# The triangular inverse of a recurrent layer on blocks of 16 instead of 32, completed by two small products

## The chip, the cores and the metric

The kernel runs on one core of a Trainium2 chip. The metric is the device time of one execution in microseconds (us), as a median of runs. A core has five engines that work through their own instruction lists in order and wait for each other by semaphores: PE (TensorE, matrix products), DVE (VectorE), ACT (ScalarE), POOL (GpSimd) and SP, which here only issues DMAs.

## What is computed

The reference is a two-layer encoder trunk on 512 positions of width 1024: layer A (RWKV-7 time mixing with 12 heads of 64, beside a four-head attention into memory tokens), layer B (chunked attention beside the same memory attention), a gated channel mixer after each, all in float32. The change lies in the recurrence of layer A:

```
def step(state, inp):
    r_t, w_t, k_t, v_t, a_t, b_t = inp
    sa = jnp.einsum('bhvk,bhk->bhv', state, a_t)
    state = (state * w_t[:, :, None, :] + sa[..., None] * b_t[:, :, None, :]
             + v_t[..., None] * k_t[:, :, None, :])
    return state, jnp.einsum('bhvk,bhk->bhv', state, r_t)
```

The kernel doesn't step through positions. It cuts the 512 positions into 8 chunks of 64 and solves each chunk at once. Within a chunk the terms `sa` depend on each other through a strictly triangular 64x64 matrix L, so that the inverse T of (identity minus L) is needed, for each chunk and each head.

## The kernel before

**Pairs and stages.** The 12 heads are worked on in 6 pairs, numbered 0 to 5; a pair's two heads lie in the upper and the lower 64 partitions. Each pair passes three generators: `prepare` (its three projections, decay, keys, and the inverse), `front` (the chunk's matrices, masked) and `back` (the completed inverse, the chunk recurrence, the output norm). A stage weaves `back` of one pair, `front` of the next and `prepare` of the one after: `weave` always continues the generator that is least far along by its share of an estimated cost, where each `yield` names a cost in ns (and perhaps a pause). What comes out of it is then put in order for each engine by a scheduler, and that order is fixed in the program. The sixth pair has no further `prepare` beside it: in the last weave its `front` and `back` run beside `back` of the fifth pair, the memory attention (`q_mem`, `mA`) and the first output projections (`out_ahead`).

**The inverse.** In `keys`, L643 makes the 64x64 matrices of all chunks in PSUM. For each head the two 32x32 blocks on the diagonal go to DRAM (`Lc`, L648 and L649) and come back with one block per partition, in four copies for four groups of columns (`Lr`, L653). DVE then solves for the inverse of all blocks at once by forward substitution over 31 steps (L656 to L668): for the first eight steps one instruction for each column group (L661), later two instructions (L666 into `Xu`, L668 into the tile `Xs`). The result goes through DRAM again (L671, L674) into the diagonal blocks of the tile `Tt`. `back` completes `Tt` from 32 to 64: it transposes blocks on DVE (`Tl`, L775), multiplies 32x32 tiles on PE (L780, into `X5`, L784; L794) and copies the off-diagonal block into `Tt` (L798). L804 uses the finished `Tt`.

**Around it.** `norm` statistics of heads go through `head_rsqrt`: L549 on PE, small instructions (L221 to L225) and L555 on DVE, L558 on PE. `front` multiplies (L716), masks (L719 on DVE), and copies on ACT (L744, L733). Weights are loaded in full precision (`wraw`, two buffers, L180 on SP) and split into two parts of lower precision: L169 on ACT, and the rest either by L175 on DVE or, between the first and the last stage, by L172 on ACT and an adding DMA on POOL's queue (L173). The dense products take both parts (L198, L199, L202), three matmuls for each block of 128 inputs. SP issues all other DMAs from one queue, in order.

In the last weave the tiles of `other_tiles` reuse buffers for the sixth pair's `back`: `AR`, and before the change `Lr` (for `MQ`) and `Xs` (for the split weight `g2h`, `g2l`).

Of the kernel before, what the change touches and what calls it, by code (L numbers as in the profile page):

```python
# [18 lines left out]
P = 128  # L19
# [20 lines left out]
for _n, _c in _VEC:  # L40
# [5 lines left out]
        ("m1", 128), ("i64", 64), ("x0", 256)]  # L46
# [8 lines left out]
def _constants():  # L55
    f = np.float32
    c = np.zeros((P, NCST), f)

    def put(name, a):
        o, n = COFF[name]  # L60
        c[:, o:o + n] = a

    i = np.arange(P)
    same = (i[:, None] // 64) == (i[None, :] // 64)
    put("ident", np.eye(P, dtype=f))
    put("ones_d", np.full((P, 2), 1.0 / 1024, f))
# [10 lines left out]
    put("x0", (np.arange(32)[None, None, :] == 4 * np.arange(8)[None, :, None] + (i // 32)[:, None, None])  # L77
        .astype(f).reshape(P, 256))
    return c
# [32 lines left out]
def trunk_kernel(ctx, tc, A, out):  # L112
# [275 lines left out]
    Tts = [lp.tile([P, NCH, 64], F32, name=f"Tt{n_}") for n_ in range(3)]  # L388
# [27 lines left out]
    xs = [kt_("Lr", (P, 32, 32))[:].rearrange("p a b -> p (a b)").rearrange("p (m s) -> p m s", m=2),  # L416
# [16 lines left out]
    for t_ in Tts:  # L433
        for h in range(2):
            GP.memset(t_[h * 64 + 32:h * 64 + 64, :, 0:32], 0.0)
# [28 lines left out]
    norm_rho(acc, rho[:])  # L464

# [99 lines left out]
    def prepare(i, T):  # L565
# [54 lines left out]
        def keys():  # L620
# [23 lines left out]
            Lc = kt_("Lc", (P, NCH, 32))  # L644
# [6 lines left out]
            Lr = kt_("Lr", (P, 32, 32))  # L651
            for g in range(4):
                nc.sync.dma_start(Lr[g * 32:g * 32 + 32], d1[:].rearrange("u c i s -> (u c) i s"))  # L653
            X = kt_("Xs", (P, 8, 32))
            V.tensor_copy(X[:].rearrange("p m i -> p (m i)"), C("x0"))
            for q in range(31):  # L656
                k, n = q // 4 + 1, 31 - q
                L1 = Lr[:, q + 1:, q:q + 1]
                if k <= 2:
                    for m in range(k):  # L660
                        V.scalar_tensor_tensor(X[:, m, q + 1:], L1[:, :, 0], X[:, m, q:q + 1], X[:, m, q + 1:],  # L661
                                               op0=ALU.mult, op1=ALU.add)
                    continue
                u = kt_("Xu", (P, 80))
                uv = u[:, 0:k * n].rearrange("p (m i) -> p m i", i=n)
                V.tensor_tensor(uv, L1.rearrange("p i o -> p o i").to_broadcast([P, k, n]),  # L666
                                X[:, 0:k, q:q + 1].to_broadcast([P, k, n]), op=ALU.mult)
                V.tensor_tensor(X[:, 0:k, q + 1:], X[:, 0:k, q + 1:], uv, op=ALU.add)  # L668
            d2 = dp.tile([4, NCH, 8, 4, 32], F32, name="d2", tag="d2", bufs=2)
            for g in range(4):  # L670
                nc.sync.dma_start(d2[:, :, :, g, :].rearrange("u c m i -> (u c) m i"), X[g * 32:g * 32 + 32])  # L671
            for u in range(4):
                rw = slice(u * 32, u * 32 + 32)
                nc.sync.dma_start(Tt[rw, :, u % 2 * 32:u % 2 * 32 + 32], d2[u].rearrange("c m g i -> (m g) c i"))  # L674
# [31 lines left out]
    def front(i, T):  # L706
        v, KB, AR, Tt = c3(T["v"][:]), T["KB"], T["AR"], T["Tt"]
# [41 lines left out]
        yield 800  # L749
        T.update(Rq=Rq, ML=ML, VT=VT)  # L750

    FRONT_COST = 2 * 1000 + 1000 + 800
# [6 lines left out]
    def other_tiles():  # L759
# [3 lines left out]
        mq = kt_("Lr", (P, 32, 32))[:].rearrange("p a b -> p (a b)").rearrange("p (c t) -> p c t", c=8)  # L763
        g = kt_("Xs", (P, 2, P), dt=F32R)
# [161 lines left out]

    def told(g, n):
# [3 lines left out]
    def ahead():  # L931
# [6 lines left out]
           (chain(front(b_, Ts[b_]), back(b_, Ts[b_], dst_mix, other_tiles, lambda: "back" in over)),  # L938
# [338 lines left out]
```

## Time and profile before

| | |
|---|---|
| median of 3 runs | 1378.8 us (1378.46 to 1378.82) |
| profiled execution: time, span | 1377.77 us, 1376.0 us |
| mean granted clock of PE | 0.987 |
| busy: PE, DVE, ACT, POOL | 1319.7 (96%), 826.9 (60%), 611.6 (44%), 34.1 (2%) us |
| where the recurrent layer lies | the first 345 us or so of the span |

All times below are in us from the start of the profiled span, unless marked ns. A row of a timeline gives start, duration, engine, source line, operation, the tiles written and read, shapes, the number of instructions merged into the row, and in brackets for how long the engine stood idle before and what ended that. A row of waits gives the waiting engine and line, what it waited for, the sum, the count and the longest. A matmul's duration contains its way through the array, so the spacing of starts tells what a matmul costs, not its duration.

### The profile page before, as it was taken

The page shows a single profiled execution, that of the slowest core. Times are in us where ns is not written, and L with a number is a line of the kernel's source. Part 1 is how long each engine was busy: PE and PEld are TensorE (multiplying, and loading weights), DVE is VectorE, ACT ScalarE, POOL GpSimd, SP SyncE. Part 2 cuts the span into 40 slices and gives each one's busy share as a digit, 9 for nine tenths or more (in the row PEclk, how much of TensorE's full clock was granted, in tenths as well). Part 3 has the DMA queues.
Part 4 walks back from the last instruction along what each step waited for, and adds up shares of the span by engine and source line. Part 5 has one row for each costly group of instructions (what it writes and reads, how often), then busy time and mean ns, then how long its engine had stood idle before and what let it go on. Part 6 is the DMA issues. An engine that isn't in the chain of part 4 may idle for free. (4 is left out here: it accounts for less than half of the span.)

```text
span 1376.0 us, 20868 instructions
## 1 busy us (share of the span) xinstructions
PE 1319.7 (96%) x8266; PEld 1071.2 (78%) x8266; DVE 826.9 (60%) x1752; ACT 611.6 (44%) x1022; POOL 34.1 (2%) x55
## 2 busy tenths in 40 slices
PE   6999999995999999999999999999999999999996
PEld 5777777774688888888888878786788888888886
DVE  7876789774666555565333667657665565563324
ACT  5556555552444333333222566657443333332321
POOL 3000000000000000000000000000000000000000
PEclk9999999997999999999999999999999999999998
DMA  5276544451042223223232422223223222222332
GB/s 181 83 208 136 109 108 110 99 142 42 24 146 92 92 94 106 92 93 102 84 98 85 152 91 74 90 92 99 93 92 103 96 93 102 98 88 85 104 94 75
DMA packets 63506, 139.18 MB, mean 101 GB/s; under 512 B 24624, under 2 KB 28336, under 8 KB 63408
## 3 DMA queue, kind: packets, MB, share of 16 engines
q1 hardware_dynamic: 60672, 127.89, 29.3%
q0 software_dynamic: 2736, 9.96, 4.2%
q8 instruction: 65, 1.06, 0.3%
q14 instruction: 33, 0.27, 0.1%
HBM read 131.01 MB, written 6.82 MB: 100 GB/s over the span
## 5 line engine op out<-in xcount | busy, mean ns | idle before, releaser
L175 DVE TENSOR_TENSOR wlo<-wraw,whi 128x1024 fp32r<-128x1024 f32 x183 | 218.9, 1197 | 128.4 <-PE psd L202 118.3
L169 ACT CAST whi<-wraw 128x1024 fp32r<-128x1024 f32 (+1 forms) x202 | 207.6, 1029 | 153.3 <-PE psd L199 38.5
L198 PE MATMUL psd<-r1h,whi 128*128 128x512 f32 x336 | 136.6, 407 | 1.3 <-ACT whi L169 1.2
L198 PE MATMUL psf<-r2h,whi 128*128 128x512 f32 x352 | 137.2, 390 | 0.0
L198 PE MATMUL psf<-r1h,whi 128*128 128x512 f32 x352 | 137.2, 390 | 0.0
L199 PE MATMUL psf<-r1l,whi 128*128 128x512 f32 x352 | 137.1, 390 | 0.0
L199 PE MATMUL psf<-r2l,whi 128*128 128x512 f32 x352 | 137.1, 390 | 0.0
L199 PE MATMUL psd<-r1l,whi 128*128 128x512 f32 x336 | 134.1, 399 | 0.0
L202 PE MATMUL psd<-r1h,wlo 128*128 128x512 f32 x336 | 92.5, 403 | 3.1 <-DMA wlo<-in_wA_dram 3.1
L199 PE MATMUL psd<-f3l,whi 128*128 128x512 f32 (+1 forms) x238 | 88.7, 377 | 0.0
L198 PE MATMUL psd<-f3h,whi 128*128 128x512 f32 (+1 forms) x238 | 88.6, 377 | 0.0
L358 DVE TENSOR_TENSOR tmp<-psf,rho 128x512 f32<-128x512 f32 x44 | 30.4, 692 | 94.7 <-PE psf L202 94.7
L202 PE MATMUL psf<-r1h,wlo 128*128 128x512 f32 x352 | 87.0, 389 | 0.0
L202 PE MATMUL psf<-r2h,wlo 128*128 128x512 f32 x352 | 86.9, 389 | 0.0
L198 PE MATMUL psd<-r2h,whi 128*128 128x512 f32 (+1 forms) x200 | 77.6, 392 | 0.1
L198 PEld LDWEIGHTS psd<-r1h,whi 128*128 128x128 f32 x336 | 63.8, 190 | 17.4 <-issue 2.4
L199 PE MATMUL psd<-r2l,whi 128*128 128x512 f32 (+1 forms) x200 | 76.4, 385 | 0.8 <-DVE r2l L215 0.8
L202 PEld LDWEIGHTS psf<-r1h,wlo 128*128 128x128 f32 x352 | 66.1, 188 | 13.7
L202 PEld LDWEIGHTS psf<-r2h,wlo 128*128 128x128 f32 x352 | 66.1, 188 | 13.7
L199 PEld LDWEIGHTS psf<-r1l,whi 128*128 128x128 f32 x352 | 66.1, 188 | 13.6
L198 PEld LDWEIGHTS psf<-r2h,whi 128*128 128x128 f32 x352 | 66.1, 188 | 13.7
L199 PEld LDWEIGHTS psf<-r2l,whi 128*128 128x128 f32 x352 | 66.1, 188 | 13.6
(352 smaller groups left out, 2429.2 us busy)
## 6 DMA issues: line engine op xcount, KB each, us to landing
wraw<-in_ffn_in_dram SPq DMA_DIRECT2D x88, 512.0 KB, 3.3
wraw<-in_ffn_out_dram SPq DMA_DIRECT2D x32, 448.0 KB, 3.3
wraw<-in_wA_dram SPq DMA_DIRECT2D x20, 512.0 KB, 4.3
wlo<-in_wA_dram POOLq DMA_DIRECT2D x17, 512.0 KB, 7.7
wraw<-in_w_out_dram SPq DMA_DIRECT2D x16, 512.0 KB, 3.8
wraw<-in_ffn_out_dram SPq DMA_DIRECT2D x16, 512.0 KB, 4.1
wraw<-in_wB_dram SPq DMA_DIRECT2D x8, 512.0 KB, 3.4
Lr<-d SPq DMA_DIRECT2D x24, 128.0 KB, 5.5
```

The lines of the kernel that those rows point to most:

```text
L169: SC.copy(hi[:, :n], raw)
L175: V.tensor_tensor(lo[:, :n], raw, hi[:, :n], op=ALU.subtract)
L198: PE.matmul(ps, wh[:, j * P:(j + 1) * P], ah, start=start and n == 0, stop=False)
L199: PE.matmul(ps, wh[:, j * P:(j + 1) * P], al, start=False, stop=False)
L202: PE.matmul(ps, wl[:, j * P:(j + 1) * P], act(k)[0], start=False, stop=stop and n == len(ks) - 1)
L358: V.tensor_tensor(v[:], pv[:], rho[:], op=ALU.mult)
```

## The change

The diagonal blocks that are solved by substitution shrink from 32 to 16 rows. The half-size inverses are put together to 32 by two products per pair, at the end of `front`:

- `Lr` has four blocks of 16 per 32-block and head in place of copies for four column groups: `Lr[P, 16, 16]`, filled by four DMAs of rows of 16 numbers (64 bytes); two copies for two column groups.
- The substitution has 15 steps: four with one instruction per column group (six instructions), eleven with two. `X` becomes a fixed tile of 48 columns, of which 16 on either side stay zero, so that a 16-block goes out as a row of 32 with zeros beside it. The start values `x0` take 128 columns instead of 256.
- The way back from DRAM feeds a second tile `Tc` beside `Tt`: eight DMAs in turn, instead of four. `Lc` and `Tc` live on until `front` (`Lc` with two buffers).
- `front` transposes `Tc` on DVE (`Tn`), multiplies `Lc` by the lower block (L770), copies (`Y`, L772), multiplies by the transposed upper block (L778) and copies the off-diagonal 16x16 blocks into `Tt` in four pieces (L781).
- The cost of `front` for the weave grows by 1600 ns; a pause of 6000 ns stands between `front` and `back` of the last pair. `other_tiles` takes `KB` and `Lr` in place of `Lr` and `Xs`. At the start, `Tts` become one tile whose first parts hold the input x for a while, so its clearing on POOL moves behind the input's norm.

```diff
-            Lr = kt_("Lr", (P, 32, 32))
-            for g in range(4):
-                nc.sync.dma_start(Lr[g * 32:g * 32 + 32], d1[:].rearrange("u c i s -> (u c) i s"))
-            X = kt_("Xs", (P, 8, 32))
-            V.tensor_copy(X[:].rearrange("p m i -> p (m i)"), C("x0"))
-            for q in range(31):
-                k, n = q // 4 + 1, 31 - q
+            Lr = kt_("Lr", (P, 16, 16))
+            for g in range(2):
+                for b_ in range(2):
+                    o, bs = g * 64 + b_ * 32, slice(b_ * 16, b_ * 16 + 16)
+                    nc.sync.dma_start(Lr[o:o + 32], d1[:, :, bs, bs].rearrange("u c i s -> (u c) i s"))
+            V.tensor_copy(X[:, :, 16:32], C("x0").rearrange("p (m i) -> p m i", i=16))
+            for q in range(15):
+                k, n = q // 2 + 1, 15 - q
...
-            d2 = dp.tile([4, NCH, 8, 4, 32], F32, name="d2", tag="d2", bufs=2)
-            for g in range(4):
-                nc.sync.dma_start(d2[:, :, :, g, :].rearrange("u c m i -> (u c) m i"), X[g * 32:g * 32 + 32])
+            d2 = dp.tile([4, NCH, 2, 8, 2, 32], F32, name="d2", tag="d2", bufs=2)
+            for g in range(2):
+                for b_ in range(2):
+                    o = g * 64 + b_ * 32
+                    nc.sync.dma_start(d2[:, :, b_, :, g].rearrange("u c m i -> (u c) m i"),
+                                      X[o:o + 32, :, 16 - b_ * 16:48 - b_ * 16])
+            Tc = kt_("Tc", (P, NCH, 32))
             for u in range(4):
-                rw = slice(u * 32, u * 32 + 32)
-                nc.sync.dma_start(Tt[rw, :, u % 2 * 32:u % 2 * 32 + 32], d2[u].rearrange("c m g i -> (m g) c i"))
+                rw, sr = slice(u * 32, u * 32 + 32), d2[u].rearrange("c b m g i -> (b m g) c i")
+                nc.sync.dma_start(Tc[rw], sr)
+                nc.sync.dma_start(Tt[rw, :, u % 2 * 32:u % 2 * 32 + 32], sr)
+            T.update(Lc=Lc, Tc=Tc)
...
+        Tn = kt_("Tn", (P, NCH, 32))
+        V.transpose(Tn[:].rearrange("p c s -> p (c s)"), Tc[:].rearrange("p c s -> p (c s)"))
+        ps = ps_s((P, 8, 16))
+        for c in range(8):
+            for u in range(4):
+                rw = slice(u * 32, u * 32 + 32)
+                PE.matmul(ps[rw, c], Lc[rw, c], Tc[rw, c, 16:32], start=True, stop=True, tile_position=(u * 32, u * 32))
+        Y = kt_("Y", (P, NCH, 16))
+        SC.copy(Y[:], ps[:])
+        yield 800, 600
+        ps = ps_s((P, 8, 16))
+        for c in range(8):
+            for u in range(4):
+                rw = slice(u * 32, u * 32 + 16)
+                PE.matmul(ps[rw, c], Tn[rw, c, 0:16], Y[rw, c], start=True, stop=True, tile_position=(u * 32, u * 32))
+        for u in range(4):
+            rw = slice(u * 32, u * 32 + 16)
+            SC.copy(Tt[rw, :, u % 2 * 32 + 16:u % 2 * 32 + 32], ps[rw])
+        yield 800
...
-           (chain(front(b_, Ts[b_]), back(b_, Ts[b_], dst_mix, other_tiles, lambda: "back" in over)),
+           (chain(front(b_, Ts[b_]), later(6000), back(b_, Ts[b_], dst_mix, other_tiles, lambda: "back" in over)),
```

The change also moves instructions in the fixed order of each engine. Three places matter below. A row gives the line, the operation, the tile written, the tiles read, the shape and the number of equal rows in a run.

The first is PE in the last weave, where the last dense product of the memory queries (L202) ends and the sixth pair's inverse is first needed. Before:

```order
L202 MATMUL psd<-r1h,wlo 128x512 x6
L830 MATMUL psl<-ML,VT 64x64 x8
L202 MATMUL psd<-r1h,wlo 128x512 x2
L780 MATMUL pss<-AR,ML 32x32
L788 MATMUL pss<-VT,ML 64x64 x12
L780 MATMUL pss<-AR,ML 32x32 x15
L788 MATMUL pss<-VT,ML 64x64 x4
L804 MATMUL pss<-VT,Tt_93 64x128 x8
L794 MATMUL pss<-Tt_94,AR 32x32 x16
```

And after, from the same six L202 on; L814 stands for L780, L838 for L804, L849 for L815, L855 for L821:

```order
L202 MATMUL psd<-r1h,wlo 128x512 x6
L770 MATMUL pss<-Tc,Lc 32x16
L864 MATMUL psl<-ML,VT 64x64 x8
L202 MATMUL psd<-r1h,wlo 128x512 x2
L770 MATMUL pss<-Tc,Lc 32x16 x31
L778 MATMUL pss<-Y,Tn 16x16 x32
L838 MATMUL pss<-VT,Tt_92 64x128 x8
L849 MATMUL pss<-ML,W 64x128 x16
L855 MATMUL pss<-VT,ML 64x64 x16
L814 MATMUL pss<-AR,ML 32x32 x16
```

The two new products stand where the sixth pair's L780 stood, and three groups of the fifth pair's `back` (L838, L849, L855) now stand ahead of L814, which had followed L780.

The second place is DVE at the head norm of the fourth pair, just before the last weave (`hra` and `rsq` are the norm's, `v` and `bon` belong to the sixth pair's `prepare`). Before, with the substitution only after the masking:

```order
L225 SCALAR_TENSOR_TENSOR rsq<-rsq_3841,rsq 128x8
L555 COPY tmp<-rsq 128x512
L856 TENSOR_TENSOR tmp<-tmp,pss 128x512
L858 TENSOR_TENSOR tmp<-tmp,bon 128x512
L719 TENSOR_TENSOR ML<-pss,cst 128x4x128
L867 TENSOR_TENSOR tmp<-tmp,psl 128x512
L719 TENSOR_TENSOR ML<-pss,cst 128x4x128 x2
L661 SCALAR_TENSOR_TENSOR Xs<-Lr,Xs 128x31
```

After, at the same norm; L560 stands for L555, L732 for L719:

```order
L224 SCALAR_TENSOR_TENSOR rsq_3980<-rsq_3980,hra 128x8
L667 SCALAR_TENSOR_TENSOR Xs<-Lr,Xs 128x15
L667 SCALAR_TENSOR_TENSOR Xs<-Lr,Xs 128x13
L667 SCALAR_TENSOR_TENSOR Xs<-Lr,Xs 128x14
L667 SCALAR_TENSOR_TENSOR Xs<-Lr,Xs 128x12
L667 SCALAR_TENSOR_TENSOR Xs<-Lr,Xs 128x13
L225 SCALAR_TENSOR_TENSOR rsq<-rsq_3980,rsq 128x8
L714 TENSOR_TENSOR bon<-pss,v 128x512
L667 SCALAR_TENSOR_TENSOR Xs<-Lr,Xs 128x12
L223 TENSOR_TENSOR rsq_3980<-rsq 128x8
L672 TENSOR_TENSOR Xu<-Lr,Xs 128x33
L224 SCALAR_TENSOR_TENSOR rsq_3980<-rsq_3980,hra 128x8
```

The substitution has moved ahead of the end of the norm: 12 of its instructions stand before L560. Its last three stand behind the fourth masking.

The third place is ACT in the last weave (`X` and `AR` are the off-diagonal blocks of the fifth and the sixth pair, `Lr` there the split weight of the sixth pair's `back`), after the change:

```order
L172 ACTIVATE wlo<-wraw 128x1024
L818 COPY X<-pss 32x256 x2
L891 ACTIVATE tmp<-tmp,vec 128x512
L823 COPY VT<-pss 128x512
L214 CAST Lr<-tmp 128x128
L757 COPY VT<-pss 128x512 x2
L832 COPY Tt_92<-pss 32x8x32 x2
L746 COPY ML<-pss 128x8x64 x2
L839 COPY W<-pss 128x256
L841 COPY VT<-pss 64x256 x2
```

Before, the cast of that weight (then into `Xs`) stood behind eight more rows, the last of them four casts of the mixed heads (`r1h`), and none of the copies here stood behind it.

More of the change, by code (lines that the diff above doesn't have):

```diff
@@ L387, in trunk_kernel @@
     E = lp.tile([P, NCH, 65], F32, name="E")
-    Tts = [lp.tile([P, NCH, 64], F32, name=f"Tt{n_}") for n_ in range(3)]
+    Tt3 = lp.tile([P, 3, NCH, 64], F32, name="Tt3")
+    Tts = [Tt3[:, n_] for n_ in range(3)]
     om = lp.tile([P, 18], F32, name="om")
@@ L432, in trunk_kernel @@
     GP.memset(E[:, :, 0:1], 1.0)
[L433 to L435 removed]
+    X = lp.tile([P, 8, 48], F32, name="Xs")
+    for o in (0, 32):
+        GP.memset(X[:, :, o:o + 16], 0.0)
     hact = pair_of(r1h, r1l)
@@ L464, in trunk_kernel @@
     norm_rho(acc, rho[:])
+    for t_ in Tts:
+        for h in range(2):
+            GP.memset(t_[h * 64 + 32:h * 64 + 64, :, 0:32], 0.0)
     GP.memset(acc[:], 1.0)
```

31 lines of the change are left out of this document (17 added, 14 removed).

## The prediction

> **What bounds the kernel now.** The page gives PE 96% busy, so I looked for the place where it is not: first at the busy time by stretch, then at PE's waits, then at the timelines around the longest. The columns of the first view are busy time and count of each engine, then PE's granted clock.
>
> ```profile
> core 0: us, PE busy (x) PEld busy (x) DVE busy (x) ACT busy (x) POOL busy (x), PEclk, DMA share, GB/s
> 98.00:102.00 4.00, 4.00 (x23) 3.10 (x22) 2.02 (x6) 1.04 (x1) 0.13 (x1) 0.61 1.06 263
> 270.00:300.00 30.00, 28.82 (x334) 21.87 (x329) 22.35 (x78) 15.79 (x27) 1.72 (x2) 1.00 0.43 87
> 326.00:331.00 5.00, 4.62 (x82) 4.08 (x82) 0.67 (x2) 1.31 (x3) 0.00 (x0) 0.50 0.11 18
> engine line waited for: us in total, times, longest us
> PE pss L780 <- DVE AR L775: 14.7, 1, 14.7
> PE psd L202 <- DMA wlo<-in_wA_dram: 3.1, 1, 3.1
> PE psl L835 <- DVE W L836: 1.8, 3, 0.7
> ```
>
> In the stages of pairs 0 to 4 PE is the limit (28.82 of 30); what leaves DVE there is worth little, and what comes to PE is paid in full. Only between 311 and 326 does PE stand still, once, 14.7 us, for the last pair's inverse. Afterwards it works at clock 0.50 until 331, so some 2.3 of those 5 us are lost too. DVE and SP show what it waited for:
>
> ```profile
> 290.65 0.17 DVE L849 TENSOR_SCALAR hra<-pss 128x8 f32<-128x8 f32 x1 [1.49 <-PE pss L549]
> 294.54 0.43 DVE L555 COPY tmp<-rsq 128x512 f32<-128x512 f32 x1
> 300.96 1.59 DVE L661 SCALAR_TENSOR_TENSOR Xs<-Lr,Xs 128x31 f32<-128x31 f32 x9
> 302.46 0.69 DVE L719 TENSOR_TENSOR ML<-pss,cst 128x512 f32<-128x512 f32 x1
> 316.26 1.23 DVE L175 TENSOR_TENSOR wlo<-wraw,whi 128x1024 fp32r<-128x1024 f32 x1
> 318.37 0.20 DVE L666 TENSOR_TENSOR Xu<-Lr,Xs 128x28 f32<-128x28 f32 x1
> 319.88 0.17 DVE L668 TENSOR_TENSOR Xs<-Xs,Xu 128x8 f32<-128x8 f32 x1
> 327.20 0.43 DVE L775 STREAM_TRANSPOSE AR<-Tt 32x256 f32<-32x256 f32 x1 [0.97 <-DMA Tt<-d]
> 320.08 2.52 SPq L671 DMA_DIRECT2D d<-Xs  x4
> 324.09 1.82 SPq L674 DMA_DIRECT2D Tt<-d  x4
> ```
>
> The substitution runs from 300.96 to 320.05. Its result then goes out to DRAM and back: first issue 320.08, read back from 324.09 (4.0 later), second transpose at 327.20.
>
> Below, names of the changed kernel's lines stand with those they had: L563 was L558, L560 was L555, L732 was L719, L757 was L744, L814 was L780, L818 was L784.
>
> **DVE's part.** Six substitutions before:
>
> ```profile
> L666 DVE TENSOR_TENSOR Xu<-Lr,Xs x138: 164/258/302, 84.9 to 319.7; 128x60 f32<-128x60 f32 x18, 128x66 f32<-128x66 f32 x12, 128x69 f32<-128x69 f32 x6, 128x63 f32<-128x63 f32 x6
> L668 DVE TENSOR_TENSOR Xs<-Xs,Xu x138: 166/220/239, 85.7 to 319.9; 128x60 f32<-128x60 f32 x18, 128x66 f32<-128x66 f32 x12, 128x69 f32<-128x69 f32 x6, 128x63 f32<-128x63 f32 x6
> L661 DVE SCALAR_TENSOR_TENSOR Xs<-Lr,Xs x72: 227/254/273, 78.0 to 303.6; 128x27 f32<-128x27 f32 x12, 128x26 f32<-128x26 f32 x12, 128x25 f32<-128x25 f32 x12, 128x24 f32<-128x24 f32 x12
> ```
>
> A sixth is 23 x 0.258 + 23 x 0.220 + 12 x 0.254 = 14.0 us. After, 11 steps of two instructions on 8 to 36 columns (0.17 to 0.21 by the rows at 318.37 and 319.88) and 6 single ones (at most 0.23): 22 x 0.19 + 6 x 0.23 = 5.6. So 8.4 us leave DVE in each pair. By themselves I cost them at nothing, since PE covers them in five of six stages (DVE 22.35 of 30 beside PE's 28.82).
>
> **PE's part.** Two new products per pair, each 32 calls on four 32x32 tiles along the diagonal; an fp32 call is two matmul instructions (16 calls show as x32), so 64 instructions each. The nearest rows:
>
> ```profile
> 256.38 1.15 PE L788 MATMUL pss<-VT,ML 64*64 64x64 f32 x32 [0.34 <-DVE ML L719]
> 257.46 0.69 PE L794 MATMUL pss<-Tt,X 32*32 32x32 f32 x32
> 258.08 0.50 PE L198 MATMUL psd<-r1h,whi 128*128 128x512 f32 x1
> 258.42 0.40 PE L199 MATMUL psd<-r1l,whi 128*128 128x512 f32 x1
> 258.65 0.39 PE L198 MATMUL psd<-r1h,whi 128*128 128x512 f32 x1
> 268.53 0.27 PE L740 MATMUL pss<-cst,AR 64*64 64x64 f32 x2
> 269.46 0.23 PE L742 MATMUL pss<-cst,v 64*64 64x64 f32 x2
> 269.62 1.15 PE L821 MATMUL pss<-VT,ML 128*64 128x64 f32 x32
> ```
>
> L794, on two tiles, takes 0.62 (257.46 to 258.08) for 32. On 64x64 tiles, two tiles take 1.08 for 32 (L788), four take 1.09 for 64 (L740 with L742, 268.53 to 269.62): four tiles work side by side. So 64 instructions on four tiles cost about 0.6, at most 1.24 if only two overlap, at least 0.3 if 16 columns instead of 32 halve it. The next dense product starts 0.34 after the first instead of 0.23: 0.11 more for each switch. A pair pays 2 x 0.7 = 1.4 (0.8 to 2.7). Pairs 0 to 4: **+7.0** (4 to 13.5).
>
> The Trainium skill speaks against this, in "TensorE: Matmul & The Clock Gate", section "Wait — 56ns, not 53.3ns?": start-to-start never falls under about 25 ns, however narrow the matmul. By it a pair would pay 3.2 us in place of 1.4. L794's 0.62 for 32 is 19 ns, so this trace already lies under that floor, on two tiles.
>
> ACT gets five small copies per pair, at most 0.37 each (two of 32x256 take 0.75, L798 below): 1.8 us beside 15.79 of 30 busy, hidden in the stages by PE's work and counted in the tail. The halved constant and the zeroing at the start are hidden as well: POOL's sums there wait 13.6 us for ACT, and the clearing that has moved fits into that wait.
>
> ```profile
> L462 POOL TENSOR_TENSOR Rq<-Rq,tmp 128x512 f32<-128x512 f32 x3 | 5.6, 1854 | 13.8 <-ACT tmp L460 13.6
> 256.83 0.69 DVE L719 TENSOR_TENSOR ML<-pss,cst 128x512 f32<-128x512 f32 x1
> 273.48 1.64 PE L202 MATMUL psd<-r1h,wlo 128*128 128x512 f32 x6
> 275.16 1.06 ACT L172 ACTIVATE wlo<-wraw 128x1024 fp32r<-128x1024 f32 x1 [1.05 <-PE psd L202]
> 82.90 1.22 DVE L175 TENSOR_TENSOR wlo<-wraw,whi 128x1024 fp32r<-128x1024 f32 x1
> 84.15 5.66 SPq L180 DMA_DIRECT2D wraw<-in_wA_dram  x3
> ```
>
> **New waits.** In four stages the order puts 12 substitution instructions ahead of L560 (L555 before), which PE's L563 needs. L555 ended at 294.97, just as PE got there. 12 x 0.18 (L661's nine in 1.59) is 2.2; two transposes of 0.43 have left the place, and PE has two dense products more to do first (0.46): up to 0.9, at least nothing. I take 0.5, **+2.0**. The first new product should wait for no DMA in the stages. Take pair 4: its substitution now ends just after the second masking (256.83 + 0.69, so 257.7), Tc lands 8.5 later by the tail's steps below, at 266.2, and L770 stands behind the six L202 that end at 275.0: 9 us of lead. If Tc were that late, everything on PE would stand behind L770, and DVE's queue behind the transpose Tn. Four more DMA issues a pair (1.8 us of SP, by L674's row) stand ahead of a weight load; that load needs a weight buffer which ACT's L172 frees only at 276.2, so they cost nothing, and 1.8 where that cover is gone.
>
> **What relief brings.** The 3.1 us wait on wlo, followed by clock 0.61 for 4 us (1.6 lost), belongs to a weight whose load SP issued at 84.15, just when DVE's L175, amid the first substitution, had read the buffer (82.90 + 1.22). Fewer instructions stand ahead of that now: nothing to 4.7, and I take a little under the middle, **-2.0**. Other waits for DVE such as L835's 1.8: **-1.5** (nothing to 3).
>
> **The tail**, on the old time axis. The substitution starts after the rsqrt row, about 291.5, and its last three instructions stand behind the fourth masking (L732, before L719, ended 303.15): end about 304. That is 16 us sooner. Three things eat of it:
>
> ```profile
> 301.70 1.07 ACT L744 COPY VT<-pss 128x512 f32<-128x512 f32 x2 [2.59 <-PE pss L742]
> 310.96 0.73 PE L202 MATMUL psd<-r1h,wlo 128*128 128x512 f32 x2
> 326.38 0.28 PE L780 MATMUL pss<-AR,ML 32*32 32x32 f32 x2 [14.69 <-DVE AR L775]
> 328.06 1.05 PE L780 MATMUL pss<-AR,ML 32*32 32x32 f32 x30
> 332.14 0.75 ACT L798 COPY Tt<-pss 32x256 f32<-32x256 f32 x2
> ```
>
> First, ACT's cast of a weight into Lr (L214) now stands ahead of the VT copies (301.70 before) and must wait until the substitution has read Lr: copies at 304.3, PE 2.3 late, dense work done at about 314.3 instead of 311.7. Secondly, the way through DRAM: 304.5 + 4.0, the seventh of eight issues (6 x 0.455), landing 1.75: Tc there at 313.0, so L770 finds it ready and ends at 315. Thirdly, the transpose Tn stands on DVE behind L912 (which needs the dense work, 0.7), two splits (0.6 each) and L175 (1.23): done at 317.9; L778 then ends at 318.5. Copies (four, at most 0.37 each) and two transposes lie beside 2.6 us of the former pair's products, with about 1 us of wait in them: L814 at 322.1. Before, its place was 328.06, with those 2.6 still to do and 1.5 still to lose at half clock. Some 2 us of new waits follow, as there is less left to fill them: 6.0 + 2.6 + 1.5 - 2.0 = **-8.1** (-3 to -14), pair 5's products included.
>
> **Sum:** 7.0 + 2.0 - 2.0 - 1.5 - 8.1 = -2.6 on the profiled execution's 1377.77. The median of the three runs, 1378.8, stands 1.0 above that, so 1376.2 on the median's scale.
>
> **Rivals.**
> *Dear small products, slower:* if tiles overlap only by two, a pair pays 2.7: 6.5 more over five pairs and 1.3 in the tail, 1384.0. The sum turns positive from 1.8 us a pair on. For it: no row here has four tiles of 32 rows, or 16 columns. Against it: L740 with L742. By the Trainium skill's 25 ns (the section named above), 3.4 with the switches, it would be 1388.
> *The whole hole closes:* ACT isn't held and Tn comes early; then 14.7 + 2.3 - 1.4 - 0.6 (one copy between the products) = 15.0 goes instead of 8.1: 1369.3. For it: 16 us of lead against 14.7. Against it: ACT's and DVE's new order.
> *The wait only moves:* L770 stands where L780 stood, and SP has a write of mixd and its read back ahead of the inverse's way out; if these land late, or the blocks of 64 bytes of Lr do, the tail keeps all but 2: 1382.3. The same name, DMA, would stand on the wait; the change would then not do what it says.
>
> **Numbers.** Forecast 0.48 (its own range 1373 to 1379: 0.24 faster, 0.22 same, 0.02 slower); dear products 0.15; hole closed 0.20; wait moved 0.12 (0.05 same, 0.07 slower); others 0.05 (0.02, 0.01, 0.02). 0.2% is 2.8 us, about what a measurement tells from no change. Faster 0.46, same 0.28, slower 0.26. From the closed hole to the dear products the range is 1369 to 1385; it leaves out the far half of each of these and part of the others.
>
> **What would show it.** L770 and L778 at about 0.6 us for 64, else the second term is wrong. PE's waits: 14.7 gone, at most 4 in L778's place, none on L770; a wait of 5 or more on L770 with DMA behind it is the third rival. Clock 1.00 between 311 and 331, else 2 us come back. The substitution's last instruction some 14 to 17 us sooner relative to pair 5's L732. If PE waits at L563 by more than 1 us per stage, DVE's order is what I misjudged.

## The result: 8.0 us less

The changed kernel takes 1370.79 us (median of eight runs, 1368.42 to 1375.42) beside 1378.81 us for the one before (eight runs, 1377.88 to 1380.51): ratio 0.9942, 95% interval 0.9929 to 0.9955. On a second chip it was 1370.31 beside 1377.63 us, ratio 0.9949 (0.9937 to 0.9962). So it is faster, by about 0.55%; 1376.2 was forecast, 5.4 more. The measured time lies inside the range of 1369 to 1385, but below the forecast's own 1373 to 1379.

Two executions of the changed kernel have a profile. The first took 1375.42 us (span 1373.6), the slowest of its eight; the second 1370.48 (span 1368.7), close to the median. Unless it says otherwise, "after" below is the second. PE's waits of the first, then of the second (waited for; us in total, times, longest):

```profile
PE pss L563 <- DVE tmp L560: 4.1, 2, 3.9
PE pss L778 <- ACT Y L772: 3.3, 2, 2.9
...
PE pss L770 <- DMA Tc<-d: 2.4, 2, 2.0
```

```profile
PE pss L778 <- ACT Y L772: 4.5, 2, 4.1
...
PE pss L770 <- DMA Tc<-d: 2.5, 2, 2.0
...
DVE Xs L667 <- DMA Lr<-d: 3.7, 1, 3.7
```

The 14.7 us wait is gone, and in its place stand 2.5 on L770 and 0.4 of the 4.5 on L778; the other 4.1 are a new wait in the first stage. Busy time by stage, first before, then after (PE, PEld, DVE, ACT, POOL; granted clock). Each window is one stage, from one pair's masked products to the next pair's; the last row of each fence is the tail:

```profile
169.30:210.40 41.10, 39.45 (x496) 30.33 (x493) 33.35 (x123) 23.76 (x44) 2.59 (x3) 1.00 0.53 114
210.40:253.30 42.90, 41.99 (x559) 32.05 (x557) 35.71 (x125) 25.49 (x46) 2.59 (x3) 1.00 0.48 103
253.30:296.20 42.90, 41.26 (x530) 31.45 (x524) 34.38 (x123) 23.36 (x43) 2.59 (x3) 1.00 0.46 104
...
311.00:331.00 20.00, 5.31 (x86) 4.33 (x84) 9.64 (x32) 2.83 (x7) 0.00 (x0) 0.57 0.29 64
```

```profile
173.20:215.00 41.80, 41.37 (x661) 32.44 (x654) 29.75 (x95) 26.00 (x51) 2.59 (x3) 1.00 0.53 105
215.00:256.80 41.80, 41.37 (x661) 32.43 (x655) 29.76 (x95) 26.03 (x51) 2.59 (x3) 1.00 0.50 101
256.80:298.60 41.80, 41.38 (x660) 32.47 (x655) 29.62 (x93) 25.60 (x50) 2.59 (x3) 1.00 0.53 112
...
311.00:331.00 20.00, 17.10 (x391) 15.12 (x390) 7.75 (x14) 8.96 (x23) 0.00 (x0) 0.83 0.18 43
```

Three stages took 126.9 us before and take 125.4 now, with 397 more instructions on PE, 384 of them the new products: its idle time in them fell from 4.2 to 1.3 us. In the tail PE is busy for 17.1 of the 20 us in which it had 5.3.

To place the time, one row is followed through all traces: DVE's eviction of a projection, L596 before and L601 after, three for each pair, always right behind the same dense work. The last of the eighteen, before and after:

```profile
287.12 0.69 DVE L596 TENSOR_TENSOR tmp<-psd,rho 128x512 f32<-128x512 f32 x1
```

```profile
289.96 0.69 DVE L601 TENSOR_TENSOR tmp<-psd,rho 128x512 f32<-128x512 f32 x1 [1.89 <-PE psd L202]
```

It comes 2.84 us later, yet the span ends 7.3 sooner (1368.7 against 1376.0), so the tail behind it is 10.1 shorter. The same subtraction for each pair's third eviction, for all kernels (us against before's trace; the names are those of the experiments). The first column lies ahead of all that PE got new, and its spread of some 2 us lies in the waits at the start, of which PE has 12.5 to 14.4 us in these executions. "Stages" is the sixth column less the first, "tail" the end less the sixth.

| kernel | pair 0 | 1 | 2 | 3 | 4 | 5 | end | stages | tail |
|---|---|---|---|---|---|---|---|---|---|
| before, start of the row | 81.63 | 120.99 | 160.14 | 202.30 | 244.19 | 287.12 | 1376.0 | | |
| after, first execution | -0.4 | +0.3 | +3.0 | +2.6 | +2.5 | +7.6 | -2.4 | +8.0 | -10.0 |
| after, second execution | +0.1 | +1.4 | +4.5 | +4.1 | +4.0 | +2.8 | -7.3 | +2.7 | -10.1 |
| no_products | -0.7 | -2.2 | -0.6 | -1.6 | -2.3 | -4.2 | -17.4 | -3.5 | -13.2 |
| products_twice | -1.4 | +1.8 | +11.4 | +17.6 | +21.9 | +27.2 | +17.4 | +28.6 | -9.8 |
| products_apart | -1.0 | +6.4 | +14.8 | +18.3 | +22.0 | +24.3 | +14.8 | +25.4 | -9.5 |
| sub_twice_last | -0.8 | -0.8 | +2.3 | +1.9 | +1.8 | +0.6 | -7.1 | +1.4 | -7.7 |
| sub_twice_rest | +0.2 | +7.8 | +7.5 | +11.1 | +15.9 | +21.3 | +16.7 | +21.1 | -4.6 |
| sub_rest_later | -0.3 | -2.1 | +3.0 | +7.8 | +11.0 | +10.7 | +0.9 | +11.0 | -9.8 |
| first_later | +0.2 | -2.1 | +4.8 | +4.4 | +4.3 | +3.1 | -7.6 | +2.9 | -10.7 |
| mixd_on_pool | +0.7 | +1.2 | +4.9 | +4.6 | +4.4 | +3.9 | -6.7 | +3.2 | -10.6 |
| lr_whole | -1.0 | -0.8 | +2.2 | +4.2 | +5.5 | +8.1 | -5.7 | +9.0 | -13.8 |
| first_mixd | -1.1 | -1.4 | +0.3 | -0.1 | -0.2 | +0.9 | -10.3 | +1.9 | -11.2 |
| all_later_mixd | -1.5 | -2.6 | +2.8 | +3.2 | +3.8 | +3.4 | -6.6 | +4.8 | -10.0 |

The change pays 2.7 us in the stages (4.4 in the first two, against 1.7 won in the other three) and wins 10.1 in the tail.

### The profile page after: what moved, and what is told of

Its sections match the earlier page's. It is cut to its first block, busy times and chain, and to the rows that moved or that the text cites. A ratio compares the mean times of both kernels' runs of the same rounds, so it can differ in the third digit from the quotient of the medians.

```text
span 1373.6 us, 22297 instructions
## 1 busy us (share of the span) xinstructions
PE 1331.2 (97%) x9034; PEld 1082.2 (79%) x9034; DVE 794.6 (58%) x1578; ACT 619.3 (45%) x1052; POOL 34.6 (3%) x57
## 5 line engine op out<-in xcount | busy, mean ns | idle before, releaser
L198 PE MATMUL psd<-r1h,whi 128*128 128x512 f32 x336 | 138.3, 412 | 1.0 <-ACT whi L169 0.9
L198 PE MATMUL psf<-r1h,whi 128*128 128x512 f32 x352 | 137.1, 390 | 0.0
L198 PE MATMUL psf<-r2h,whi 128*128 128x512 f32 x352 | 137.1, 390 | 0.0
L202 PE MATMUL psd<-r1h,wlo 128*128 128x512 f32 x336 | 92.5, 403 | 0.0
L198 PE MATMUL psd<-f3h,whi 128*128 128x512 f32 (+1 forms) x238 | 88.5, 376 | 0.0
L202 PE MATMUL psf<-r1h,wlo 128*128 128x512 f32 x352 | 87.0, 389 | 0.0
L202 PE MATMUL psf<-r2h,wlo 128*128 128x512 f32 x352 | 86.9, 389 | 0.0
L198 PEld LDWEIGHTS psd<-r1h,whi 128*128 128x128 f32 x336 | 63.9, 190 | 18.5 <-issue 3.0
L198 PE MATMUL psd<-r2h,whi 128*128 128x512 f32 (+1 forms) x200 | 77.6, 391 | 0.1
L202 PEld LDWEIGHTS psf<-r1h,wlo 128*128 128x128 f32 x352 | 66.1, 188 | 13.7
L202 PEld LDWEIGHTS psf<-r2h,wlo 128*128 128x128 f32 x352 | 66.1, 188 | 13.7
L198 PEld LDWEIGHTS psf<-r2h,whi 128*128 128x128 f32 x352 | 66.1, 188 | 13.7
L198 PEld LDWEIGHTS psf<-r1h,whi 128*128 128x128 f32 x352 | 66.0, 188 | 13.6
```

The lines of the kernel that those rows point to most:

```text
L198: PE.matmul(ps, wh[:, j * P:(j + 1) * P], ah, start=start and n == 0, stop=False)
L202: PE.matmul(ps, wl[:, j * P:(j + 1) * P], act(k)[0], start=False, stop=stop and n == len(ks) - 1)
```

## The experiments

All start from the changed kernel. The order on each engine is fixed when the kernel is built, from priorities and estimated times, so an edit also shifts rows elsewhere: in no_products, products_apart, sub_twice_rest, sub_rest_later and all_later_mixd over a hundred of PE's rows are moved, added or gone, in the others a few tens at most. Times are medians with the lowest and the highest run, ratios go to the kernel before on the same chip, with 95% intervals.

| run | us | ratio |
|---|---|---|
| after_again | 1370.31 (1368.74 to 1371.98) | 0.9949 (0.9937 to 0.9962) |
| no_products | 1363.81 (1360.48 to 1367.57) | 0.9894 (0.9879 to 0.9909) |
| products_twice | 1396.53 (1395.02 to 1398.42) | 1.0145 (1.0127 to 1.0163) |
| products_apart | 1392.57 (1389.62 to 1393.71) | 1.0101 (1.0085 to 1.0118) |
| sub_twice_last | 1372.79 (1370.01 to 1378.34) | 0.9966 (0.9954 to 0.9977) |
| sub_twice_rest | 1395.00 (1389.56 to 1402.37) | 1.0130 (1.0106 to 1.0154) |
| sub_rest_later | 1378.81 (1374.97 to 1381.39) | 1.0005 (0.9994 to 1.0017) |
| all_later_mixd | 1376.75 (1371.20 to 1382.46) | 0.9994 (0.9981 to 1.0007) |
| first_later | 1369.95 (1367.55 to 1370.15) | 0.9931 (0.9920 to 0.9943) |
| mixd_on_pool | 1369.84 (1368.32 to 1371.10) | 0.9935 (0.9923 to 0.9947) |
| first_mixd | 1368.84 (1366.64 to 1370.68) | 0.9932 (0.9918 to 0.9946) |
| lr_whole | 1371.62 (1366.36 to 1375.37) | 0.9947 (0.9929 to 0.9965) |

**The same kernel again.**

> The changed kernel once more, for a second profile, since the first profiled execution took 1375.42 us and the median of eight is 1370.79 us. Theory 1 (the waits on Lr and the tail wait on Tc come and go with how long the DMAs took): this execution is about 1371 us, and the 7.8 us of DVE's waits on Lr and the 4.1 us of PE's waits at L563 are smaller by some 3 to 5 us. Theory 2 (those waits stand in every execution, the 4.6 us lie spread over the span): the same rows come again within 0.5 us.

Theory 1. The first execution lost its 5 us at one place, the last stage of the table (+2.5 to +7.6): Lr came late, the substitution stood ahead of L560, and L560 ahead of PE's L563. PE's clock over the wait and just behind it, 256 to 262, was 0.61. DVE's row and PE's:

```profile
254.79 0.81 DVE L667 SCALAR_TENSOR_TENSOR Xs<-Lr,Xs 128x15 f32<-128x15 f32 x5 [4.03 <-DMA Lr<-d]
...
258.22 1.12 PE L563 MATMUL pss<-cst,tmp 128*128 128x128 f32 x4 [3.93 <-DVE tmp L560]
```

In the second execution Lr is late once, in the first pair, and L563 waits for nothing worth a row. The waits in the first stage and at L770 came again.

**The products: left out, doubled, doubled in two bursts.**

```diff
 no_products
-                PE.matmul(ps[rw, c], Lc[rw, c], Tc[rw, c, 16:32], ...)
-        Y = kt_("Y", (P, NCH, 16))
-        SC.copy(Y[:], ps[:])
...
-                PE.matmul(ps[rw, c], Tn[rw, c, 0:16], Y[rw, c], ...)
...
-            SC.copy(Tt[rw, :, u % 2 * 32 + 16:u % 2 * 32 + 32], ps[rw])
 products_twice
-                PE.matmul(ps[rw, c], Lc[rw, c], Tc[rw, c, 16:32], ...)
+                for _ in range(2): PE.matmul(ps[rw, c], Lc[rw, c], Tc[rw, c, 16:32], ...)
...
-                PE.matmul(ps[rw, c], Tn[rw, c, 0:16], Y[rw, c], ...)
+                for _ in range(2): PE.matmul(ps[rw, c], Tn[rw, c, 0:16], Y[rw, c], ...)
 products_apart
+        ps = ps_s((P, 8, 16))
...
+                PE.matmul(ps[rw, c], Lc[rw, c], Tc[rw, c, 16:32], ...)
+        yield 800, 600
...
+        ps = ps_s((P, 8, 16))
...
+                PE.matmul(ps[rw, c], Tn[rw, c, 0:16], Y[rw, c], ...)
+        yield 800
...
-    FRONT_COST = 2 * 1000 + 1000 + 3 * 800
+    FRONT_COST = 2 * 1000 + 1000 + 5 * 800
```

> The two small products, the copies of their results and Y are left out (the lower left 16x16 blocks of the inverse are not completed), Tc, Tn and all the rest kept; the order of the rest shifts in places. Theory 1 (the sum of the prediction: a product is paid where PE sets the pace): 5 x 1.4 = 7.0 us less in the stages and in the tail the 1.5 us from the last Tc to the end of L778, and the 4.1 us wait at L778 of the first stage: 1370.3 - 12.6 = 1357.7 us. Theory 2 (the products mostly fill time that PE would have idled): less than 4 us gained, above 1366 us.

> Each instruction of the two new products issued twice: 128 more per pair, which the trace has at 0.62 to 0.66 us per 64. Theory (PE sets the pace in the stages, so a product is paid in full): 5 x 1.3 = 6.4 us for the first five pairs and 1.3 for the sixth, 1370.8 + 7.7 = 1378.5 us. Rival (the products lie in holes that PE has anyway, before L563 and L778): under 3 us more, below 1374 us.

> Each product computed twice, as in the run that took 1396.5 us, but the second time as a burst of its own with dense work between, so that no burst has over 64 instructions but where two lie next to each other. Theory 1 (128 short instructions in a row run PE out of its instruction stream: the 11 us of waits on issue and the slow clock behind them come from the length of a burst): the waits on issue go, 1370.3 + 7.7 + 5 switches of 0.1 x 2 = 1379 us. Theory 2 (the number of small instructions in the stage counts, however spread, or the shifted order): above 1390 us.

In the last of the three, nothing reads the results of the second bursts.

Without the products: 6.5 us less by the medians and up to 7.6 by the ratios, between the two theories. By the table they cost 6.2 in the stages (+2.7 against -3.5) and 3.0 in the tail, but this profiled execution was the fastest of its five, 3.3 us under their median. What is left, the short substitution with all the rest of the change, stands 14.9 us ahead of before (1363.81 against 1378.74): -3.5 in the stages and -13.2 in the tail. That is the value of the short substitution together with the new order, of which some 7 are paid back for the products.

Doubling them missed both theories: +26.2 us, not 7.7. PE's timeline in the third stage shows a part of it:

```profile
158.05 1.19 PE L778 MATMUL pss<-Y,Tn 16*16 16x16 f32 x118
162.19 0.30 PE L778 MATMUL pss<-Y,Tn 16*16 16x16 f32 x10 [2.95 <-issue]
...
163.05 0.79 PE L198 MATMUL psd<-r1h,whi 128*128 128x512 f32 x1
```

After 118 short instructions PE stands for 2.95 us in the middle of one product, waiting for nothing that the profile shows, and then works at half clock (0.50 from 163 to 165, L198 at 0.79). Four such stops at L778 make 7.4 us in all. In two bursts they shrink to 1.2, as theory 1 had it, but the time falls only to 1392.6: other waits took their place.

```profile
PE pss L554 <- ACT tmp L629: 6.1, 1, 6.1
PE pss L770 <- DMA Tc<-d: 3.0, 1, 3.0
PE pss L850 <- ACT Tt L844: 3.0, 3, 1.0
...
PE pss L784 <- issue: 0.9, 1, 0.9
```

So theory 2 by its number. The 6.1 at L554 are the first stage; in each of the last three stages this kernel lies 3.5 to 3.9 us behind the change, of which 1.3 are the instructions and 1.0 the wait at L850; the remaining 1.2 to 1.6 I cannot place. Twice the work is no clean dose here.

**The substitution: twice in the last pair, twice in the others.** The diff is that of sub_twice_last; sub_twice_rest has `i < NPAIR - 1` in its place.

```diff
-            V.tensor_copy(X[:, :, 16:32], C("x0").rearrange("p (m i) -> p m i", i=16))
-            for q in range(15):
+            for q in [*range(15)] * (2 if i == NPAIR - 1 else 1):
+                if q == 0: V.tensor_copy(X[:, :, 16:32], C("x0").rearrange("p (m i) -> p m i", i=16))
```

> The substitution of the last pair done twice from its start value, some 5.7 + 0.3 us more of DVE, the other five as in the change. Theory 1 (the end of this substitution sets the products and with them the tail): +6.0 us, 1376.8 us, the wait before L770 grown from 2.4 to about 8 us. Theory 2 (the way out is held on SP by the read of mixd, which comes 3.3 us after the substitution ends): 6.0 - 3.3 = +2.7 us, 1373.5 us. Theory 3 (the tail was not what the change won): within 1 us of 1370.8.

> The substitution of the first five pairs done twice, some 6.0 us more of DVE each, the last as in the change. Theory 1 (DVE's time in the stages is covered by PE, only L563 behind L560 feels it): up to 1 us per stage, 1371 to 1376 us. Theory 2 (the shorter substitution is worth most of its time in the stages too): 5 x 6.0 = up to 30 us, above 1385 us.

In the last pair: +2.5 us in the median, and the same in the table's tail (-7.7 against -10.1). Theory 2, which gave +2.7. The rows of the change, then of this kernel (end of the substitution on DVE; SP's read of mixd, in the change with its wait, and first issue of the way out; PE's second product). This kernel's trace lies 2.3 us earlier here, by the last eviction (287.70 against 289.96):

```profile
304.74 0.17 DVE L674 TENSOR_TENSOR Xs<-Xs,Xu 128x8 f32<-128x8 f32 x1
...
SPq L921 <- DMA mixd<-tmp: 4.6, 1, 4.6
...
307.34 0.32 SPq L921 DMA_DIRECT2D tmp<-mixd  x1
307.75 1.86 SPq L680 DMA_DIRECT2D d<-Xs  x4
...
318.75 0.73 PE L778 MATMUL pss<-Y,Tn 16*16 16x16 f32 x64 [0.35 <-ACT Y L772]
```

```profile
308.87 0.17 DVE L674 TENSOR_TENSOR Xs<-Xs,Xu 128x8 f32<-128x8 f32 x1
...
305.17 0.32 SPq L921 DMA_DIRECT2D tmp<-mixd  x1
309.07 1.80 SPq L680 DMA_DIRECT2D d<-Xs  x4
...
318.37 0.72 PE L778 MATMUL pss<-Y,Tn 16*16 16x16 f32 x64 [0.36 <-ACT Y L772]
```

In the change the result is ready at 304.91 and leaves at 307.75: SP's queue is held by the read of mixd, which waits for its write. Done twice, the substitution ends at 309.04 and leaves at once. The last 2.8 us that the change won on DVE are therefore lost on SP.

In the other five: +24.7 us, far nearer to theory 2, and PE waits for Tc at L770 in stage after stage:

```profile
PE pss L770 <- DMA Tc<-d: 11.6, 7, 4.1
```

Of the 11.6 us, 7.2 lie in the stages, which lose 18.4 against the change, and 4.4 in the tail, which loses 5.5 although nothing in it was doubled: the last substitution ends 21.8 us behind the last eviction there, 15.0 in the change. The rest of the loss isn't placed; part of it is slow clock (0.96 in the fourth and the fifth stage).

That could be DVE's time itself or the early place of the products. The next run puts the products later:

```diff
         rows_kb()
-        yield 800
+        yield 800, (9000 if i < NPAIR - 1 else 0)
```

> The first five substitutions done twice, as in the run that took 1395.0 us, and the two products of these five pairs put off by 9 us of the weaving's own time. In the second profile of the changed kernel Tc of pair 3 has landed by 231.8 (its transpose starts) and L770 comes at 236.1, a lead of 4.3 us, less than the 6.0 us that the second pass takes. Theory 1 (the products' early place makes a deadline, and the second pass overran it): with 9 us more of lead the loss goes, 1370 to 1376 us. Theory 2 (DVE's time itself is short in the stages: L560, L732 and the next pair's keys stand behind it): stays within 4 us of 1395.

16.2 of the 24.7 us come back (17.2 by the ratios), which speaks for theory 1, though 1378.8 lies 2.8 above its range. Part of what is left is the late place itself. The nearest run that has the same late products and single substitutions is all_later_mixd below: 1376.75. With lead, then, the five second passes, some 30 us of DVE, cost 2.1 us (1.5 by the ratios, whose intervals overlap). That run also has the read of mixd on POOL, and as the late place makes the kernel slower by itself, some of DVE's time may hide behind that: that PE covers DVE's time once there is lead is likely, not shown.

The deadline can be read in the change. Tn begins when Tc has landed and its turn on DVE has come. In pair 1 DVE waited for Tc, and PE's L770 came at 151.99, a lead of 0.9 us; in pair 3 L770 came at 236.14, a lead of at least 4.3, some 16 us after the substitution's end (219.6). All are less than the 6.0 us of a second pass.

```profile
151.06 0.45 DVE L765 STREAM_TRANSPOSE Tn<-Tc 128x256 f32<-128x256 f32 x1 [1.31 <-DMA Tc<-d]
...
231.79 0.44 DVE L765 STREAM_TRANSPOSE Tn<-Tc 128x256 f32<-128x256 f32 x1
```

In the first stage and in the last one the late place takes back nearly all that the second pass had cost (table); in the three between it does not. In the third and the fourth the trace shows where: from 201 to 215 PE is busy, but at a granted clock of 0.52, nearly 7 us lost, where the change has 1.00. Just before, the late products stand among the small matmuls of the recurrence (L869, L874), and the longest of PE's waits there is 0.6 us.

```profile
201.00:215.00 14.00, 13.80 (x100) 0.52 0.40 70
```

**The first stage.** The new 4.1 us wait hangs on ACT and a weight load. The rows of the change: SP issues two weight loads, ACT's cast waits for the first, Y's copy stands three rows behind that cast, and PE behind Y.

```profile
99.92 0.83 SPq L180 DMA_DIRECT2D wraw<-in_wA_dram  x2
...
106.24 1.04 ACT L169 CAST whi<-wraw 128x1024 fp32r<-128x1024 f32 x1 [3.52 <-DMA wraw<-in_wA_dram]
...
109.09 0.28 ACT L772 COPY Y<-pss 128x128 f32<-128x128 f32 x1
...
109.42 0.73 PE L778 MATMUL pss<-Y,Tn 16*16 16x16 f32 x64 [4.13 <-ACT Y L772]
```

```diff
         rows_kb()
-        yield 800
+        yield 800, (0 if i else 9000)
```

> The two products of the first pair alone are put off by 9 us of the weaving's own time, so that PE reaches L770 after Tc has long landed; order elsewhere in the stages as in the change. In the second profile of the changed kernel PE waits 4.1 us at L778 in the first stage and runs at a granted clock of 0.89 between 90 and 120 us. Theory 1 (this hole is new time): 4.1 us and up to 2 us of slower clock go, -3 to -6 us, 1364.5 to 1367.5 us. Theory 2 (pair 1's keys wait for the same DVE and DMA work anyhow, the hole moves to L563 or L729): within 1 us of 1370.3.

The wait goes (of 4.5 us at L778, the tail's among them, 0.9 are left) and the first stage is 3.6 us shorter than in the change, but in this execution the second stage is 3.8 longer: a new 2.3 us wait of L838 for ACT's copy of Tt, and from 131 to 138 a clock of 0.51. The change has such a stretch behind its own hole (0.57 from 108 to 116). 1369.95 us lies under the change's medians; the intervals overlap (0.9920 to 0.9943 against 0.9929 to 0.9955). Unclear, nearer to theory 2.

**SP's queue in the tail.**

```diff
-            nc.sync.dma_start(t_[:], mixd[m])
+            (GP if m == 3 else nc.sync).dma_start(t_[:], mixd[m])
```

> The read of the fourth mixd tile (L921) issued from POOL in place of SP; nothing else moved but a few weight-residual matmuls around the first pieces of L770. In the second profile of the changed kernel the last substitution ends at 304.91, yet its way out is issued at 307.75, behind that read, which waits for its own write till 307.34. Theory 1 (that wait on SP is paid): Tc comes 2.8 us sooner, PE's 2.5 us before L770 go, and what is left is Tn, on DVE behind a weight residual that ends at 317.5: L778 could start at 318.0 in place of 318.75, so -0.8 us, 1369.5 us. Theory 2 (Tn's place doesn't bind, DVE runs ahead): -2.5 us, 1367.8 us. Theory 3 (the transfers themselves, not the queue): 0, 1370.3 us.

The mechanism is that of theory 1: the way out leaves right behind the substitution, and Tn, behind the residual of a weight on DVE, is what PE then waits for:

```profile
305.81 0.17 DVE L674 TENSOR_TENSOR Xs<-Xs,Xu 128x8 f32<-128x8 f32 x1
...
306.00 2.87 SPq L680 DMA_DIRECT2D d<-Xs  x4
...
317.99 1.22 DVE L175 TENSOR_TENSOR wlo<-wraw,whi 128x1024 fp32r<-128x1024 f32 x1
...
319.71 0.87 PE L778 MATMUL pss<-Y,Tn 16*16 16x16 f32 x64 [2.93 <-DVE Tn L765]
```

Its gain is not shown: against the last eviction L778 starts 0.1 us sooner than in the change, not 0.75, the tail is 0.5 us shorter, and the intervals of the two kernels overlap, so the time doesn't tell theory 1 from theory 3. PE's dense work and DVE's queue now end 3.5 us apart (316.1 and 319.6), with Tc landed before both: to take one wait away brings little.

**Lr in whole rows.**

```diff
-            d1 = dp.tile([4, NCH, 32, 32], F32, name="d1", tag="d1", bufs=2)
+            d1 = dp.tile([2, 4, NCH, 16, 16], F32, name="d1", tag="d1", bufs=2)
...
-                nc.sync.dma_start(d1[u].rearrange("c i s -> i c s"), Lc[rw])
+                for b_ in range(2):
+                    o, s0 = u * 32 + b_ * 16, b_ * 16
+                    nc.sync.dma_start(d1[b_, u].rearrange("c i s -> i c s"), Lc[o:o + 16, :, s0:s0 + 16])
...
-            for g in range(2):
-                for b_ in range(2):
-                    o, bs = g * 64 + b_ * 32, slice(b_ * 16, b_ * 16 + 16)
-                    nc.sync.dma_start(Lr[o:o + 32], d1[:, :, bs, bs].rearrange("u c i s -> (u c) i s"))
+            for g in range(2):
+                nc.sync.dma_start(Lr[g * 64:g * 64 + 64], d1[:].rearrange("b u c i s -> (b u c) i s"))
```

> Only the two 16x16 diagonal blocks of each 32x32 block go through DRAM, laid out so that each partition of Lr reads one run of 1 KB in place of 16 runs of 64 bytes; eight writes and two reads in place of four and four. Theory 1 (the many 64-byte pieces make Lr late, and its lateness is what makes executions differ): the 3.7 us of DVE's wait on Lr in the first stage fall to under 2, the profiled execution shows no Lr wait of 4 us before the last stage, median -1 to -3 us (1367 to 1369), the runs lie closer together than 7 us. Theory 2 (Lr's time is queueing and fixed latency, four more writes on SP cost what the reads save): within 1 us of 1370.3.

Theory 2: no faster, the runs no closer together (9.0 us), and DVE still waits for Lr:

```profile
DVE Xs L667 <- DMA Lr<-d: 4.1, 2, 3.5
```

Longer pieces in the reads didn't bring Lr sooner. As four writes more stand on SP, and the writes now go in pieces of 64 bytes (128 before), this doesn't clear the pieces: what makes Lr late is open. The loss in the stages (+9.0) and the shorter tail (-13.8) were not followed further.

**Two together.** The edits of first_later and mixd_on_pool, then mixd_on_pool with the late place for five pairs:

> The products of the first pair put off by 9 us, and the read of the fourth mixd tile on POOL: the sum of two runs that gave 0.9931 and 0.9935 against 0.9942 to 0.9949 for the change. Theory 1 (they add): 0.9942 - 0.0011 to 0.0018 - 0.0007 to 0.0014, about 0.992, 1368 us. Theory 2 (both were within the scatter of the runs): 1370 us.

> The products of the first five pairs put off by 9 us, and the read of the fourth mixd tile on POOL. Theory 1 (lead is what the stages lack; a late Lr no longer reaches PE): the first pair's hole goes as in the run with the first pair alone (-1 to -2 us), the read brings -0.8 us, runs lie closer together, 1366 to 1368 us. Theory 2 (the lead in the other pairs was enough, and products among the recurrence's small matmuls cost switches): no better than the first pair alone, 1369 us or more.

first_mixd has the lowest median of the kernels that compute everything, 1368.84 us, 0.0010 to 0.0017 under the change's two ratios; the intervals overlap, so it isn't shown to be faster than the change. The two edits don't add: its ratio, 0.9932, is that of first_later alone (0.9931), which leaves theory 2. All five products late costs some 6 us more than the change in the median. Its profiled execution, 1371.20 us, was the fastest of twelve, so its trace doesn't show the whole of that; the slow clock of sub_rest_later, with the same late products, is the nearest hint. Theory 2 by the number, with a cause that stays open.

## Why the prediction was right, and where it was off

**Price of a product: right.** About 0.6 us for 64 was forecast. Each product with the row behind it:

```profile
151.99 0.73 PE L770 MATMUL pss<-Tc,Lc 32*32 32x16 f32 x64
152.65 0.33 PE L869 MATMUL psl<-W,MQ 64*64 64x64 f32 x4
...
156.98 0.69 PE L778 MATMUL pss<-Y,Tn 16*16 16x16 f32 x64
157.60 0.33 PE L869 MATMUL psl<-W,MQ 64*64 64x64 f32 x4
```

From start to next start 0.66 and 0.62 us, so the rival of dear products falls. The +7.0 of the first five pairs measured +6.2 (the change against no_products), though not evenly: 2.8 in the first stage, with its new hole, 1.5 in the second, 0.6 to 0.7 in each of the others, half a pair's price. So the price of a product was right, but not that PE pays it in full: in the last three stages only half of it shows (PE idles 0.4 us in each with the products, 0.8 without), and that the sum came so near is luck, by a hole that nobody had foreseen.

**DVE's part: right in size, its worth bound to a condition.** The sixth of the rows is 11 x (0.204 + 0.190) + 6 x 0.226 = 5.7 us, forecast 5.6:

```profile
L672 DVE TENSOR_TENSOR Xu<-Lr,Xs x66: 164/204/221, 78.5 to 304.5; 128x30 f32<-128x30 f32 x18, 128x33 f32<-128x33 f32 x6, 128x36 f32<-128x36 f32 x6, 128x32 f32<-128x32 f32 x6
L674 DVE TENSOR_TENSOR Xs<-Xs,Xu x66: 159/190/199, 78.7 to 304.7; 128x30 f32<-128x30 f32 x18, 128x33 f32<-128x33 f32 x6, 128x36 f32<-128x36 f32 x6, 128x32 f32<-128x32 f32 x6
L667 DVE SCALAR_TENSOR_TENSOR Xs<-Lr,Xs x36: 219/226/236, 77.4 to 295.3; 128x13 f32<-128x13 f32 x12, 128x12 f32<-128x12 f32 x12, 128x15 f32<-128x15 f32 x6, 128x14 f32<-128x14 f32 x6
```

"By themselves I cost them at nothing, since PE covers them" holds with lead, as far as the runs tell (2.1 us for 30 us of DVE), and not without (24.7 us). The 9 us of lead that were worked out for the first product in pair 4 were 0.9 in pair 1 and at least 4.3 in pair 3 of the second execution. The prediction had named what follows if Tc is late; it had not asked how near it was to that.

**Relief: right as far as shown.** -2.0 and -1.5 were taken; no_products, which has the relief without the products, is 3.5 us shorter than before over the five stages, and none of the waits that the prediction priced is left. As that execution was 3.3 us under its kernel's median, the equal numbers are luck in part.

**New waits: the first term that failed.** +2.0 was taken for L563 behind L560. The second execution has none of it, the first 3.9 at once, when Lr was late. It is an event that comes in some executions (2.0 us in that of first_mixd), not 0.5 in each stage; beside the second execution the term is nothing. With it the stages come to +5.5 in the forecast and +2.7 in the trace.

**The tail: -8.1 against -10.1.** On the old time axis (less 2.84) L814 stands at 322.5; forecast 322.1. The way there was another. ACT's hold at the cast into Lr cost PE 0.49 us, not 2.3. Tn ended at 315.1, not 317.9. Against that SP let the result out 2.8 late and took 2.00 us for one issue of Tc, so L770, which was to find Tc ready, waited 2.5: the third rival's mechanism, at a small price. And from the end of L778 to L814 it took 5.9 us, not 3.6: the clock was not 1.00, but 0.50 from 318 to 322 and 0.83 over the twenty us. That these errors cancel to 0.4 us is luck.

```profile
305.57 0.71 PE L743 MATMUL pss<-cst,KB 64*128 64x64 f32 x15 [0.49 <-ACT VT L757]
...
313.86 2.00 SPq L685 DMA_DIRECT2D Tc<-d  x1
...
316.59 0.23 PE L770 MATMUL pss<-Tc,Lc 32*32 32x16 f32 x2 [2.01 <-DMA Tc<-d]
317.36 1.03 PE L770 MATMUL pss<-Tc,Lc 32*32 32x16 f32 x58 [0.54 <-DMA Tc<-d]
...
325.34 0.69 PE L814 MATMUL pss<-AR,ML 32*32 32x32 f32 x32
```

What failed in the sum is again a term for new waits, the 2.0 behind L814: from there to the end the change takes 1043.4 us and before, from 328.06, 1047.9. That is 4.6 less, where 2.6 + 1.5 - 2.0 = 2.1 was forecast; without the 2.0 it would have been 4.1.

**The sum.** -2.6 forecast, -7.3 between the two profiled executions: 2.8 of the difference in the stages, 2.0 in the tail. Without the two guesses of 2.0 for new waits the forecast would have been 1372.2. The measured time is nearer to that of the second rival, the closed hole (1369.3). Its two conditions did come true, ACT hardly held and Tn early, but the gain of 15.0 that it put in place of 8.1 did not: the wait at L770 and the slow clock left 10.1, and the stages gave the rest.

**Not foreseen:** the first stage. The five copies on ACT were called hidden, but one of them, Y's, has PE behind it and stands on ACT behind a cast that waits for a weight.

## What to carry to other kernels

When a slow step is shortened by giving its remainder to the engine that sets the pace, price both from single rows, and then ask when the remainder is wanted: a consumer that stands early leaves little lead to cover the step, and here five second passes on DVE cost 24.7 us with little lead and some 2 with more, in a kernel that the later place had itself made some 6 us slower. A copy of 0.3 us is only hidden if nothing that waits stands ahead of it on its engine. Waits that no row shows are better left to the range than put into the sum.

## What the runs showed of the hardware

Short products on small tiles were cheap: 64 instructions on four tiles of 32 rows in 0.62 to 0.66 us, 10 ns each. The Trainium skill, "TensorE: Matmul & The Clock Gate", section "Wait — 56ns, not 53.3ns?", has 25 ns as the least from start to start; these rows, of instructions that go to four tiles in turn, lie under it.

The clock fell after short waits. In the tail the longest was 2.0 us, with one of 0.5 behind it, and the clock of the four us that followed was 0.50:

```profile
318.00:322.00 4.00, 3.65 (x114) 0.50 0.40 137
```

The Trainium skill, in the same page's section "HAM oscillation — how this bites in real kernels", warns of gaps over some 3.4 us. These are shorter, and in sub_rest_later the 14 us at 0.52 followed small products with no wait over 0.6 us. The same products in the last three stages of the change left the clock at 1.00. What sets the clock back in these places no run here isolates.

PE can stop within one product with no wait that the profile shows (2.95 us after 118 short instructions in a row, 2.0 us once in first_mixd with single products). The queue of instruction transfers moved 77 packets in products_twice and 71 in the change, but also 77 in products_apart, where such stops came to 1.2 us. That these stops are instructions arriving late is a guess; no run tells.
